# Down projection of a hybrid decoder block: when the weights of its second block of features are loaded and split

## The chip, the cores and the metric

The kernel runs on one core of one Trainium2 chip. The metric is the device time of one execution in microseconds; lower is better. TensorE (PE in the profile) multiplies matrices, VectorE (DVE) and ScalarE (ACT) work on the tiles, GpSimd (POOL) does a few small operations, and SyncE (SP) issues nearly all the transfers. SP is one queue: a transfer whose wait is not yet met holds back every transfer behind it.

## The reference

One decoder block on `x` of 1024 tokens by 1024 features in float32: an attention mixer and a retention mixer read the same normalised input, are gated, merged and projected, and then a squared-ReLU MLP follows. The change lies in the last product of the MLP:

```python
xn2 = rmsnorm(x, norm2_g[l])
x = x + jnp.square(jax.nn.relu(xn2 @ w_up[l])) @ w_down[l]
```

`w_up` is 1024 x 4096 and `w_down` 4096 x 1024.

## The kernel before

**Numbers as pairs.** Each float32 operand is split into a high part (`ACT ACTIVATE`, a copy to fp32r, line 354) and a low part (`DVE TENSOR_TENSOR`, source minus high part, line 357). A product is then three matmuls: high with high, high with low, low with high (line 257).

**The down projection.** The 4096 features are cut into 8 blocks of 512 (`c`, the code's "chunk"), the tokens into 4 pairs of tiles (`t`). A unit `u` is one `(c, t)`, so there are 32 units, four to a block. Each unit is one step of Strassen's scheme: seven products N1 to N7, each of two matmul triples, so 42 matmuls of 128x512. The order in a unit (line 1326) is N6, N5, then N1 of the *next* unit, N7, N2 of the next unit, N3, N4. N1 and N2 of the very first unit stand inside the up projection's last unit (lines 1306 to 1310). In the profile a matmul of the down projection has `xh` or `xl` as its second operand. N1 of blocks 0, 2, 4 and 6 reads the buffer shown as `wh`/`wl`, N1 of blocks 1, 3, 5 and 7 the buffer `y1ah`/`y1al`.

**Rows.** The left operands of a unit, called rows here, were written to DRAM by the up projection (`h_d<-hs`, line 1243) and come back as two transfers of 896 KB, `xh<-h_d` and `xl<-h_d` (`load_rows`, lines 1252 to 1260). Three places rotate, so the rows of unit u+3 are loaded into the place of unit u when unit u has been multiplied. They are first needed at N1 of unit u+3, which stands third in unit u+2.

**Weights.** A block's weights are four quarters of 512 KB (`raw<-in_w_down`, line 210), in four places of their own. From them come the seven operands: three are a quarter itself, four are a sum or a difference of two quarters, made in place (line 186, shown as `raw<-raw,raw`). Each operand is then split into its own buffer. `add_chunks` writes this down as seven steps, in the order N1, N2, N3, N5, N7, N6, N4. The buffers of the even and of the odd blocks are two disjoint sets (lines 400 to 402). Three buffers of the odd set lie in a pool `y1`, opened after the up projection (line 1312), three in a pool `w1` (line 1321).

**Who decides when.** `Weights.pump` writes a step into the program as soon as the buffer that it fills is marked free and its quarters are loaded; `load` writes the load of a quarter as soon as the step that last used the place has been written. `free` marks buffers and calls `pump`. This gives only the order in which the program is *written*. PE keeps that order (line 306). On the other engines, SP's queue included, a planner at compile time orders the instructions: at each point of its own model of time it takes, among those whose inputs and buffers are ready, the one written first. `keep_in_program_order` adds an edge that puts an instruction behind the one written just before it on its engine. After planning, each engine's order is fixed.

**Around the change.** When the last unit of the up projection is done, the loads of block 1's quarters have been written, and opening `y1` and `w1` (lines 1317 and 1324) lets all seven steps of block 1 be written at once, ahead of the loop over the units; the loads of block 2's quarters follow in the same call.

Of the kernel before, what the change touches and what calls it, by code (L numbers as in the profile page):

```python
# [37 lines left out]
class Weights:  # L38
# [9 lines left out]
    RAW = 3  # L48
    A, B, C, D = (0, 1), (2, 3), 5, 4

    def __init__(self, nc, rawp, wp, split):
        self.nc, self.rawp, self.wp, self.split = nc, rawp, wp, split
        self.raw, self.used, self.next = [], set(), 0
        self.src, self.steps = [], []
        self.place, self.more, self.most = [], None, None
        self.last = {}
        self.units, self.done = {}, set()
        self.plain = self.taken = 0
        self.cycle, self.turn = tuple(range(self.WB)), 0

        self.places = {}

    def claim(self, buf, key):

# [105 lines left out]
    def add_chunks(self, tag, srcs, buffers):  # L170


        for c, quarters in enumerate(srcs):
            base = len(self.src)
            self.place += [(base + i) % (self.RAW + 1) for i in range(4)]
            self.src += quarters
            x00, x10, x11, x01 = range(base, base + 4)
            for name, r, other, op, ends in (
                    ("N1", x00, None, None, ()), ("N2", x10, None, None, ()), ("N3", x11, None, None, ()),
                    ("N5", x00, x01, OP.subtract, ()), ("N7", x01, x11, OP.subtract, (x01,)),  # L180
                    ("N6", x11, x00, OP.add, (x00,)), ("N4", x10, x11, OP.subtract, (x10, x11))):
                buf, key = buffers[c % 2][name], (tag, c, name)

                def step(r=r, other=other, op=op, ends=ends, buf=buf, key=key):
                    if other is not None:
                        self.nc.vector.tensor_tensor(self.raw[r], self.raw[r], self.raw[other], op=op)
                    h, l = self.buffer(buf)
                    self.split(h, l, self.raw[r])
                    self.units[key] = h, l
                    self.used.update(ends)  # L190

                self.steps.append((self.claim(buf, key), x01, step))
# [5 lines left out]

    def load(self):
        n = len(self.raw)  # L200
        if n >= len(self.src):
            return False
        b = self.place[n]
        if any(self.place[m] == b and m not in self.used for m in range(max(0, n - 16), n)):
            return False
        from_ = self.rawp if b < self.RAW else self.more if b == self.RAW else self.most
        if from_ is None:
            return False
        raw = from_.tile([P, UW], F, name=f"raw{b}", bufs=1)
        self.nc.sync.dma_start(raw[:, :self.src[n].shape[1]], self.src[n])  # L210
        self.raw.append(raw)
        return True
# [22 lines left out]

    def free(self, *ids):
        self.done.update(ids)
        self.pump()


class Pipe:
# [24 lines left out]
    def step(self, ps, terms, ends=None, first=True):  # L266
        fns = self.due.pop(self.slot, [])
        n, m = len(terms), len(fns)
        place = {}
        for j, fn in enumerate(fns):  # L270
            place.setdefault(min(n - 1, (j + 1) * n // (m + 1)), []).append(fn)

        def after(i):
            for fn in place.get(i, []):
                fn()
            if ends and i in ends:
                ends[i]()

        self.group(ps, terms, after, first)
        self.slot += 1  # L280
# [9 lines left out]
def strassen_order(units):  # L290


    order = [(0, "N1"), (1, "N1"), (0, "N2"), (1, "N2")]
    for j in range(units):
        late = j + 3 >= units
        order += [(j, "N6"), (j, "N5")] + ([] if late else [(j + 2, "N1")]) + [(j, "N7")]
        order += [(j, "N3")]
        order += [(j + 2, "N2")] if not late else [(units - 1, ("N1", "N2")[j + 3 - units])] if j + 1 < units else []
        order += [(j, "N4")]
    return order  # L300
# [3 lines left out]
def hybrid_block(ctx: ExitStack, tc: tile.TileContext, a: dict, out: bass.AP):  # L304
    nc = tc.nc
# [6 lines left out]
    rawp = pool(ctx, "rawp", 1)  # L312
    wp = pool(ctx, "wp", 1)
# [60 lines left out]
        return (slice(0, 512), slice(512, 1024))  # L374


    W = Weights(nc, rawp, wp, split)
    heads = [(slot, g) for slot in range(SLOTS) for g in (1, 2, 0)]
    for u in range(4):
        W.add(a["w_av"][u])  # L380
# [136 lines left out]
    with ExitStack() as ph:  # L517
# [96 lines left out]
        for n, t in enumerate(TILES):  # L614
# [9 lines left out]
            ends = {2 * i + 1: (lambda i=i: W.free(us[i])) for i in range(4)} if n == NT - 1 else None  # L624
            pipe.step(pm, terms, ends)
            c = px.tile([P, 512], F, name="c", bufs=1)
# [59 lines left out]
    for u in range(len(TOKEN)):  # L686
        n1, part = {}, {}
        for name in ("N1", "N2", "N6", "N5", "N3", "N7", "N4"):
            for t in range(4):
# [13 lines left out]
                elif name == "N2":  # L703
                    c = cp.tile([P, 512], F, name="c")
# [409 lines left out]
    with ExitStack() as ph:  # L1114
# [41 lines left out]
        def load_rows(n):  # L1156

            nb, t = order[n]
            ts = slice(t * P, (t + 1) * P)
            xt = pn.tile([P, 512], F, name="xr")  # L1160
            nc.sync.dma_start(xt, a["x"][ts, halves()[nb]])
            y0 = None
            if nb == 1:
                y0 = pn.tile([P, 512], F, name="y0")
                nc.sync.dma_start(y0, out[ts, :512])
            ahead.append((xt, y0))
# [34 lines left out]
    with ExitStack() as ph:  # L1201
# [60 lines left out]
        def down(u, name):  # L1262
# [28 lines left out]
            if t == 3:  # L1291
                W.free(("dn", c, name))

        for j, name in strassen_order(NU):
            product("up", j, name, unit, OP7, temps, result)
            if j == NU - 1:
                if name == "N1":
                    load_rows(0)
                if name == "N2":
                    parts = [x.rearrange("p a b -> p (a b)") for x in OP7[name]]  # L1300
                    for i, part in enumerate("ab"):
                        W.places["n2" + part] = [x[:, 1024 * i:1024 * i + 1024] for x in parts]
                    W.free(("place", "n2"))
                if name == "N5":
                    load_rows(1)
                if name == "N7":
                    down(0, "N1")
                if name == "N3":
                    load_rows(2)
                    down(0, "N2")  # L1310
# [3 lines left out]
        Y.update({r: y1.tile([P, D], F, name=f"Y{r}") for t in (1, 3, 2) for r in (t, t + 4)})  # L1314
        for x in "abc":
            W.places["y1" + x] = [y1.tile([P, UW], R, name=f"y1{x}{i}") for i in "hl"]
        W.free(("place", "y1"))


    with ExitStack() as ph:  # L1320
        w1 = pool(ph, "w1", 1)
        for x in "abc":
            W.places["w1" + x] = [w1.tile([P, UW], R, name=f"w1{x}{i}") for i in "hl"]
        W.free(("place", "w1"))
        for u in range(len(units)):
            for name, later in (("N6", False), ("N5", False), ("N1", True), ("N7", False), ("N2", True),
                                ("N3", False), ("N4", False)):
                if u + later < len(units):
                    down(u + later, name)
            load_rows(u + 3)  # L1330
    sumst.close()


# [106 lines left out]
```

## Time and profile before

| | us |
|---|---|
| median of 3 runs | 2235.59 |
| lowest and highest run | 2232.65 and 2236.57 |
| the profiled execution | 2232.95 |
| its span, first to last instruction | 2231.2 |

The down projection's first product begins at 1898.69 us of the span and the span ends at 2231.2 us. In the views, a row of the timeline is: start in us, duration in us, engine, line, operation, result and operands, count, and in brackets the idle time of the engine before it and what ended that idle time. `SPq` is SyncE issuing a transfer: its duration is the issue, not the transfer. `x` or `w` with an `h` or `l` at the end are the high and low parts.

### The profile page before, as it was taken

The numbers are of one execution on the slowest core, as the hardware profiler recorded it, in microseconds if no ns is written. First come the engines' busy times: TensorE is split into PE (matmuls) and PEld (weight loads), VectorE is DVE, ScalarE is ACT, GpSimd is POOL, SyncE is SP. The second block draws the span as 40 slices with busy tenths as digits, with TensorE's granted clock in tenths as the row PEclk, the third lists the DMA queues.
The fourth block names the chain that finished last, engine by engine and source line by source line (L and its number), as shares of the span: only waits on it lengthen the run. The fifth ranks groups of instructions, "written<-read, shape, count | busy, mean of one in ns | idle before, by whom it ended". The sixth has DMA issues, their size and how long they took to land.

```text
span 2231.2 us, 28546 instructions
## 1 busy us (share of the span) xinstructions
PE 2182.3 (98%) x10064; PEld 1792.3 (80%) x10064; DVE 1435.4 (64%) x2543; ACT 1110.6 (50%) x1936; POOL 196.6 (9%) x184
## 2 busy tenths in 40 slices
PE   8999999999999999999999999999899999899998
PEld 6788788888788887888888788888788888688887
DVE  7766675455555556657767752453877778776863
ACT  6433444477844467745545532122577777522210
POOL 3314453000000000010000000000000000000002
PEclk9999999999999999999999999999999999999999
DMA  7344433544545555364333484554378889966658
GB/s 228 99 132 114 132 114 114 158 145 146 171 149 170 160 155 161 127 207 139 117 102 111 151 283 151 174 180 146 99 223 248 248 248 282 328 248 238 248 223 174
DMA packets 345664, 392.78 MB, mean 176 GB/s; under 512 B 34737, under 2 KB 270897, under 8 KB 345266
## 3 DMA queue, kind: packets, MB, share of 16 engines
q1 hardware_dynamic: 343026, 386.25, 55.0%
q0 software_dynamic: 2496, 4.72, 1.4%
q8 instruction: 79, 1.29, 0.2%
q14 instruction: 63, 0.52, 0.1%
HBM read 252.39 MB, written 138.51 MB: 175 GB/s over the span
## 4 chain that ended last, share of the span: by engine, by line
PE 81%; DVE 6%; ACT 4%; DMA 3%; issue 3%; POOL 2%; SPq 0%; POOLq 0%; ACTq 0%; DVEq 0%
PE mm L257 46%; PE ms L257 29%; DVE wl L357 1%; PE tr L792 1%; PE tr L811 1%; DMA xl<-h_d 1%; DMA raw<-in_w_att_q 1%; ACT wh L354 1%; PE tr L650 1%; DVE xl L357 1%; POOL x L555 1%; PE tr L804 1%; PE ms L934 1%; PE tr L990 1%; ACT xh L354 1%
## 5 line engine op out<-in xcount | busy, mean ns | idle before, releaser
L357 DVE TENSOR_TENSOR wl<-raw,wh 128x1024 fp32r<-128x1024 f32 (+1 forms) x292 | 332.3, 1143 | 175.2 <-ACT wh L354 173.4
L354 ACT ACTIVATE wh<-raw 128x1024 fp32r<-128x1024 f32 (+1 forms) x292 | 287.4, 988 | 253.1 <-PE ms L257 122.1
L257 PE MATMUL mm<-xh,wh 128*128 128x512 f32 x896 | 346.8, 410 | 1.9 <-ACT wh L354 1.2
L257 PE MATMUL mm<-xl,wh 128*128 128x512 f32 x896 | 329.5, 391 | 1.7 <-DVE xl L357 1.7
L257 PE MATMUL mm<-xh,wl 128*128 128x512 f32 x768 | 301.2, 392 | 0.5 <-DVE wl L357 0.5
L257 PE MATMUL mm<-wh,xh 128*128 128x512 f32 x736 | 296.3, 403 | 0.8 <-ACT ms L1279 0.6
L257 PE MATMUL mm<-wh,xl 128*128 128x512 f32 x736 | 288.6, 392 | 4.5 <-DMA xl<-h_d 4.5
L257 PE MATMUL mm<-wl,xh 128*128 128x512 f32 x736 | 287.6, 391 | 0.0
L257 PE MATMUL ms<-xh,wh 128*128 128x512 f32 x544 | 225.6, 415 | 1.8 <-DVE St L981 1.2
L257 PE MATMUL ms<-xh,wl 128*128 128x512 f32 x544 | 212.9, 391 | 0.0
L257 PE MATMUL ms<-xl,wh 128*128 128x512 f32 x544 | 212.4, 390 | 0.0
L257 PEld LDWEIGHTS mm<-xh,wh 128*128 128x128 f32 x896 | 169.2, 189 | 34.4 <-ACT wh L354 1.6
L257 PEld LDWEIGHTS mm<-xl,wh 128*128 128x128 f32 x896 | 169.3, 189 | 31.8 <-DVE xl L357 2.1
L257 PEld LDWEIGHTS mm<-xh,wl 128*128 128x128 f32 x768 | 144.6, 188 | 32.4 <-DVE wl L357 1.0
L257 PEld LDWEIGHTS mm<-wh,xl 128*128 128x128 f32 x736 | 138.4, 188 | 35.1 <-DMA xl<-h_d 5.4
L257 PEld LDWEIGHTS mm<-wh,xh 128*128 128x128 f32 x736 | 138.7, 188 | 27.2 <-ACT ms L1279 1.0
L257 PEld LDWEIGHTS mm<-wl,xh 128*128 128x128 f32 x736 | 138.8, 189 | 25.8
L257 PE MATMUL ms<-wh,xh 128*128 128x512 f32 x336 | 137.0, 408 | 6.0 <-DVE c L705 3.4
L257 PE MATMUL ms<-wh,xl 128*128 128x512 f32 x336 | 133.3, 397 | 2.5 <-DVE xl L357 2.5
L257 PE MATMUL ms<-wl,xh 128*128 128x512 f32 x336 | 132.5, 394 | 0.8 <-DVE wl L357 0.8
L257 PEld LDWEIGHTS ms<-xh,wh 128*128 128x128 f32 x544 | 102.5, 188 | 21.9 <-DVE St L981 1.6
L257 PEld LDWEIGHTS ms<-xh,wl 128*128 128x128 f32 x544 | 102.1, 188 | 22.0
(284 smaller groups left out, 3816.4 us busy)
## 6 DMA issues: line engine op xcount, KB each, us to landing
h_d<-hs SPq DMA_DIRECT2D x112, 512.0 KB, 4.2
xh<-h_d SPq DMA_DIRECT2D x32, 896.0 KB, 6.1
xl<-h_d SPq DMA_DIRECT2D x32, 896.0 KB, 7.3
raw<-in_w_att_q SPq DMA_DIRECT2D x48, 512.0 KB, 4.2
raw<-in_w_up SPq DMA_DIRECT2D x32, 512.0 KB, 3.7
raw<-in_w_down SPq DMA_DIRECT2D x32, 512.0 KB, 5.2
qk_d<-T SPq DMA_DIRECT2D x48, 256.0 KB, 3.5
raw<-in_w_gate_q SPq DMA_DIRECT2D x16, 512.0 KB, 4.4
```

The source lines that it names most:

```text
L257: self.nc.tensor.matmul(ps, x, y, start=start, stop=stop, skip_group_check=not first)
L354: hi = nc.scalar.activation(dst_h, src, AF.Copy)
L357: nc.vector.tensor_tensor(dst_l, src, dst_h.bitcast(F), op=OP.subtract)
L555: nc.gpsimd.tensor_tensor(x[v], x[v], x[u], op=op)
L650: nc.tensor.transpose(pt[:, i, :], c[:, i * P:(i + 1) * P], ident)
L792: nc.tensor.matmul(sp[:, :w], q[:, e * P:(e + 1) * P], k[:, k0 * P:k0 * P + w], start=True, stop=True)
L804: nc.tensor.transpose(tb[:, j * P:(j + 1) * P], st["p"][:, j * P:(j + 1) * P], ident)
L811: nc.tensor.matmul(po[:, :DH], st["t"][:, j * P:(j + 1) * P], v[:, k0 + j, :], start=(j == 0), stop=(j == nk - 1))
L934: nc.tensor.matmul(sp[:, :P], kT[:, f], qT[:, f], start=(f == 0), stop=(f == 1))
L990: nc.tensor.transpose(pt[:, f, :], it["o"][:, f * P:(f + 1) * P], ident)
```

## The change

Four things are changed.

1. While the up projection writes its program, quarters of block 1 and later are not loaded: `limit` is the first quarter of block 1.
2. Opening `y1` and `w1`, and freeing a buffer, no longer writes steps: `eager` is off.
3. In units 1, 2 and 3, after each product, `ease` raises the limit by one quarter (up to the end of block 1) and lets at most one step be written. So the four loads are written after the first four products of unit 1, the steps N1, N2, N3 and N5 after its products 4 to 7, and N7, N6 and N4 after the first three products of unit 2.
4. In the steps of block 1 alone the high part's activation and the sum or difference are kept in program order. The loads and the low part are not.

After unit 3, and behind the loading of the rows of unit 6, limit and `eager` are reset and `pump` runs: block 2's four loads and seven steps are written there at once. From then on everything is as before.

```diff
+        self.limit, self.eager = None, True
+        self.bases = {}
...
         for c, quarters in enumerate(srcs):
-            base = len(self.src)
+            base = self.bases[tag, c] = len(self.src)
...
-                def step(r=r, other=other, op=op, ends=ends, buf=buf, key=key):
+                def step(r=r, other=other, op=op, ends=ends, buf=buf, key=key, pinned=c == 1):
                     if other is not None:
-                        self.nc.vector.tensor_tensor(self.raw[r], self.raw[r], self.raw[other], op=op)
+                        d = self.nc.vector.tensor_tensor(self.raw[r], self.raw[r], self.raw[other], op=op)
+                        if pinned:
+                            self.tc.keep_in_program_order(d)
                     h, l = self.buffer(buf)
-                    self.split(h, l, self.raw[r])
+                    self.split(h, l, self.raw[r], pinned)
...
     def load(self):
         n = len(self.raw)
-        if n >= len(self.src):
+        if n >= (len(self.src) if self.limit is None else self.limit):
             return False
...
     def free(self, *ids):
         self.done.update(ids)
-        self.pump()
+        if self.eager:
+            self.pump()
+
+    def ease(self, last):
+
+        if self.limit is not None:
+            self.limit = min(self.limit + 1, last)
+        self.pump(1)
...
+        W.limit = W.bases["dn", 1]
         for j, name in strassen_order(NU):
             product("up", j, name, unit, OP7, temps, result)
...
+        W.eager = False
         W.free(("place", "y1"))
...
                 if u + later < len(units):
                     down(u + later, name)
+                if 0 < u < 4:
+                    W.ease(W.bases["dn", 2])
             load_rows(u + 3)
+            if u == 3:
+                W.limit, W.eager = None, True
+                W.pump()
```

More of the change, by code (lines that the diff above doesn't have):

```diff
@@ L49, with __init__ @@
     A, B, C, D = (0, 1), (2, 3), 5, 4
-    def __init__(self, nc, rawp, wp, split):
-        self.nc, self.rawp, self.wp, self.split = nc, rawp, wp, split
+    def __init__(self, tc, rawp, wp, split):
+        self.tc, self.nc, self.rawp, self.wp, self.split = tc, tc.nc, rawp, wp, split
         self.raw, self.used, self.next = [], set(), 0
@@ L374, in halves @@
         return (slice(0, 512), slice(512, 1024))
-    W = Weights(nc, rawp, wp, split)
+    W = Weights(tc, rawp, wp, split)
     heads = [(slot, g) for slot in range(SLOTS) for g in (1, 2, 0)]
```

## The prediction

> **What bounds the kernel now.** The page comes first: it says which engine sets the time and where that engine has holes.
>
> ```profile
> span 2231.2 us, 28546 instructions
> ...
> PE 2182.3 (98%) x10064; PEld 1792.3 (80%) x10064; DVE 1435.4 (64%) x2543; ACT 1110.6 (50%) x1936; POOL 196.6 (9%) x184
> ...
> PE   8999999999999999999999999999899999899998
> ...
> DMA  7344433544545555364333484554378889966658
> ```
>
> PE sets the time: it is busy for 98% of the span. So a change is worth what it takes out of PE's holes, or adds to them. A slice is 2231.2 / 40 = 55.8 us. The "8" in slice 34 (from 1897 us, counting from 0) is the start of the down projection, and the DMA row has its highest digits just there and ahead of it. The waits of PE from 1905 us to the end say for what it waits:
>
> ```profile
> PE mm L257 <- DMA xl<-h_d: 6.9, 3, 3.1
> PE ms L257 <- ACT Y L1286: 1.0, 1, 1.0
> ```
>
> Three waits for rows, not for weights. The timeline of PE places them; with the last line of each wait I show the first matmul of N1 of the units 1 to 6, as marks, and a line of the chain of work for the undisturbed pace.
>
> ```profile
> 1910.46 0.39 PE L257 MATMUL mm<-wh,xh 128*128 128x512 f32 x1
> 1921.27 0.39 PE L257 MATMUL mm<-wh,xh 128*128 128x512 f32 x1
> 1924.99 0.50 PE L257 MATMUL mm<-wh,xl 128*128 128x512 f32 x1 [3.11 <-DMA xl<-h_d]
> 1934.57 0.47 PE L257 MATMUL mm<-wh,xh 128*128 128x512 f32 x1 [0.21 <-DMA xh<-h_d]
> 1936.67 0.50 PE L257 MATMUL mm<-wh,xl 128*128 128x512 f32 x1 [1.40 <-DMA xl<-h_d]
> 1947.49 0.39 PE L257 MATMUL mm<-y1ah,xh 128*128 128x512 f32 x1
> 1950.47 0.50 PE L257 MATMUL mm<-y1ah,xl 128*128 128x512 f32 x1 [2.36 <-DMA xl<-h_d]
> 1961.26 0.39 PE L257 MATMUL mm<-y1ah,xh 128*128 128x512 f32 x1
> 1971.27 0.39 PE L257 MATMUL mm<-y1ah,xh 128*128 128x512 f32 x1
> ...
> 1974.16 2.72 PE mm L257 x12
> ```
>
> Twelve matmuls take 2.72 us, so a product of six takes 1.36 us and a unit of 42 takes 9.52 us. From N1 to N1 the units took 10.81, 13.30, 12.92, 13.77 and 10.01 us. What is above 9.52 is lost: 1.29, **3.78 (stall 1, rows of unit 2), 3.40 (stall 2, rows of unit 3), 4.25 (stall 3, rows of unit 4)** and 0.49; in all 13.21 us. After 1971 us the chain is PE alone until its tail. Why the rows are late stands in SP's timeline:
>
> ```profile
> 1907.96 1.14 SPq L210 DMA_DIRECT2D raw<-in_w_down  x1
> 1909.19 0.53 SPq L1259 DMA_DIRECT2D xh<-h_d  x1
> ...
> 1916.46 1.09 SPq L1259 DMA_DIRECT2D xl<-h_d  x1
> ...
> 1919.81 6.09 SPq L210 DMA_DIRECT2D raw<-in_w_down  x3
> 1926.00 0.38 SPq L1259 DMA_DIRECT2D xh<-h_d  x1
> 1926.47 0.51 SPq L1259 DMA_DIRECT2D xl<-h_d  x1
> 1931.44 0.32 SPq L1259 DMA_DIRECT2D xh<-h_d  x1
> 1938.39 5.43 SPq L210 DMA_DIRECT2D raw<-in_w_down  x4
> 1943.92 0.38 SPq L1259 DMA_DIRECT2D xl<-h_d  x1
> ...
> SPq L210 <- DVE raw L186: 8.7, 2, 6.6
> ```
>
> The quarters of block 1 are the raw loads at 1907.96 (one) and 1919.81 (three), those of block 2 the four at 1938.39. Stall 2: the rows of unit 3 could be asked for when N4 of unit 0 is done, two products ahead of 1921.27, so near 1918.6, but the three raw loads hold SP until 1925.9. Stall 3: the rows' high part for unit 4 goes at 1931.44; then SP waits 6.6 us (last row, the waits of SP) for DVE to be done with a sum of block 1, issues four raw loads, and only then the low part, 12.5 us after the high one. Stall 1: the low part for unit 2 stands behind stores of the up projection's last results (left out here) which wait for DVE; one raw load went ahead of them.
>
> **The change part by part.**
>
> *Stall 3 goes: 4.25 us.* Block 2's four loads are now written behind the loading of the rows of unit 6, so rows of units 4, 5 and 6 that are ready come first. And their places are freed by block 1's steps N7, N6 and N4, now written in unit 2, whereas the rows of unit 4 are asked for at the end of unit 1. The low part then follows its high part by some 0.4 us, as in the pair at 1926, is issued near 1932 and needed 12.2 us later (nine products of 1.36 us); even the 8.5 us that the low part of 1916.46 took (to 1924.99) would do. I take 4.25; the ends are 0 and 4.25.
>
> *Stall 2 goes: 3.40 us.* Three loads leave the place ahead of the rows of unit 3. If they are issued where they are written, in unit 1, SP is free near 1919.8 and the pair goes some 6 us earlier, against waits of 0.21 + 1.40 us and what they bring behind them. Ends 0 (loads still early, first rival) and 3.40. I take 3.40, because the rows of unit 3 need only be first by 2 us.
>
> *Stall 1: no change.* The low part is held by the stores, which the change doesn't touch. If the load at 1907.96 is gone, 512 KB less lie ahead of it. The windows give the price:
>
> ```profile
> 1908.00:1936.00 28.00, 22.95 (x98) 17.76 (x96) 15.37 (x21) 16.71 (x27) 0.00 (x0) 1.00 1.04 348
> 1936.00:1941.00 5.00, 4.33 (x12) 3.43 (x13) 5.00 (x5) 2.79 (x4) 0.00 (x0) 0.66 0.47 175
> ...
> 1920.20:1923.60 3.40, 1.68 (x8) 1.06 (x6) 0.00 (x0) 1.10 (x2) 0.00 (x0) 1.00 0.99 326
> ...
> 1933.80:1937.20 3.40, 1.78 (x7) 0.91 (x6) 3.12 (x4) 2.49 (x3) 0.00 (x0) 1.00 0.92 371
> 1937.20:1940.60 3.40, 3.40 (x9) 2.63 (x8) 3.40 (x4) 1.54 (x2) 0.00 (x0) 0.51 0.33 120
> ```
>
> Columns are the window, its length, busy time of PE, PEld, DVE, ACT and POOL, then granted clock, DMA share and GB/s. From 1908 to 1936 the transfers are full (share 1.04) at 348 GB/s, so 512 KB are 1.5 us; behind that, SP's waits leave them half idle (0.47), which is where room for the moved loads comes from. Bounds: a gain of 3.78 (stall gone) to a loss of 1.67, explained next. I take 0, nearest to the row of the low part, whose issue does not move.
>
> The loss is the clock. Each of the other two stalls is followed by a stretch of 3.4 us at a granted clock of 0.51 (last two rows): 3.4 x 0.49 = 1.67 us, part of the 3.40 and the 4.25 above. It came after a window with PE busy for 1.78 of 3.40 us; after the window at 1920.20, with 1.68 us, it didn't come. So a stall 1 that stays may cost one more such stretch. [...]
>
> *Loads of block 1 in unit 1: 0.* Four times 512 KB, one per product. They now lie ahead of the rows of unit 4: 2 MB at 348 GB/s are 6.0 us, the rows themselves (1.8 MB) 5.3 us, in all 11.3 of the 12.2 us. Cover is thin; if it is gone, the cost is 1 us or, with the slow stretch, 2.7.
>
> *Steps of block 1 in units 1 and 2, pinned on ACT and DVE: 0.* The same 7 activations, 7 low parts and 4 sums as before, later. Unit prices from a later, undisturbed part:
>
> ```profile
> 1994.33 1.23 DVE L357 TENSOR_TENSOR w1al<-raw,w1ah 128x1024 fp32r<-128x1024 f32 x1 [0.41 <-ACT w1ah L354]
> ...
> 1995.59 0.33 SPq L210 DMA_DIRECT2D raw<-in_w_down  x1
> ...
> 1998.79 1.22 DVE L186 TENSOR_TENSOR raw<-raw,raw 128x1024 f32<-128x1024 f32 x1
> 1999.92 0.68 DVE L1288 TENSOR_TENSOR Y<-Y,ms 128x512 f32<-128x512 f32 x1
> 2000.04 4.93 SPq L210 DMA_DIRECT2D raw<-in_w_down  x3
> 2000.04 1.06 ACT L354 ACTIVATE w1bh<-raw 128x1024 fp32r<-128x1024 f32 x1 [3.02 <-DVE raw L186]
> 2000.52 1.22 DVE L186 TENSOR_TENSOR raw<-raw,raw 128x1024 f32<-128x1024 f32 x1
> ...
> DMA to landing us min/median/max: 3.9/5.0/10.2
> ```
>
> An activation is 1.06 us, a low part 1.23, a sum 1.22 and a result added to Y 0.68. The edge adds a wait on ACT: behind a pinned activation whose quarter has not landed stand the copies of N1's result (line 1279), and N2 waits for those, one product (1.36 us) after N1. The first step is written three products (4.1 us) after its load, which lands in 5.0 us in the middle case and 10.2 at the most (last row, the view of the raw tiles). A wait of 0.9 us is hidden by that product, one of 6.1 would cost 6.1 - 1.4 = 4.7. I take 0, by the middle case. The first use of the block is N1 of unit 4, third in unit 3, over a unit after the last step: nothing waits there.
>
> *Block 2 all at once after unit 3: 0.* Seven steps are 7 x 1.23 + 4 x 1.22 = 13.5 us of DVE; a unit's six results are 4.1 of its 9.52 us. Block 2 is first needed at N1 of unit 8, 3.3 units or 31 us later, where DVE has 31 - 13 = 18 us free. The rows above show a like burst with results of Y between the steps and PE undisturbed. The bad end is the rival below.
>
> **Sum.** -3.40 - 4.25 = -7.65 us. On the profiled execution that is 2232.95 - 7.65 = 2225.3 (its span 2231.2 and 1.75 around it). That execution lies 2.64 us below the median of the runs, 2235.59; from the median the forecast is 2227.94, so **2228**.
>
> **Rivals.**
>
> *The loads don't move.* Loads are not pinned, and SP's order is not the written one. In the rows above, the load at 1995.59 leaves just after the low part of N7 (to 1995.56) frees its place, 4.5 us ahead of three loads of which at least one, that into the place freed by N6's sum at 1999.92, was written before it. Block 1's places are free before unit 1, so its loads can still go ahead of the rows of unit 3. Against it: they now are written behind those rows, and the stores left out between SP's rows were written ahead of them too. Then stall 2 stays and 4.25 us are gained: 2231.3, or up to 1.2 us less since block 1's first low part (1.23 us) no longer stands ahead of the last stores: 2231.
>
> *The next rows are late instead.* Block 1's 2 MB meet the rows of unit 4 and stall 3 comes back whole, for the thin cover named above; only 3.40 are gained: 2232.2. For it speaks the full DMA share until 1936, against it the half idle time behind.
>
> *Slower: DVE's queue is filled with block 2 at the end of unit 3.* If the planner, trusting early landings, puts the eleven operations of block 2 ahead of unit 4's results, N7 waits for N6's result, with only two products (2.7 us) between: 13.5 - 2.7 = 10.8 us, and up to 10.2 more for the last quarter's landing, on which N5's difference waits; I take half of that, 5. Net +15.9 - 7.65: 2243.8. It is slower by 0.2% from 12.1 us on (7.65 + 4.5). Against it stands the mixing in the rows above; but there the quarters had landed long before.
>
> **How the numbers follow.** Forecast 0.50, loads that don't move 0.25, next rows late 0.13, slower 0.12. The range: 2224 is the forecast with stall 1 gone too (2227.9 - 3.8); upward it takes in the first two rivals and stops short of the slower one, which is left out: 2234. A measurement of this kernel can tell about 0.2%, 4.5 us, from no change. Faster by that: the forecast, less 0.03, and a little over half of the first rival, 0.61. Within: the rest of these two and the second rival, 0.27. Slower: 0.12.
>
> **What would show it.** Right: SP's timeline has the two parts of the rows of units 3 and 4 back to back, raw loads behind them; the waits of PE on `xl<-h_d` shrink from 6.9 us to stall 1's 3.1; granted clock 1.00 from 1930 on; N1 to N1 is 9.5 us from unit 3 on. Wrong: three or four raw loads in one piece ahead of the rows of unit 3 (first rival), a wait for `xl` at N1 of unit 4 (second), or waits of PE on `DVE Y` or `ACT ms` in units 2 to 5 (pins, or block 2's burst).

## The result, and the profile after

| | before | after |
|---|---|---|
| median | 2234.64 us (20 runs, 2230.43 to 2239.49) | 2230.41 us (20 runs, 2225.44 to 2236.36) |
| ratio | | 0.9981, 95% interval 0.9974 to 0.9987 |
| profiled execution | 2232.95 us | 2233.11 us |
| its span | 2231.2 us | 2231.0 us |

The change gains 4.2 us of the 7.65 that were forecast, 0.19%. The interval is clear of 1, but the gain is just under the 4.5 us (0.2%) that the prediction took as the least that can be told from no change. The two profiled executions are equally long all the same, so the page alone shows nothing. The page of the kernel after:

```profile
span 2231.0 us, 28539 instructions
...
PE   8899999999999999999999999999999999999998
```

The slice that held an "8" at the start of the down projection (34, counting from 0) now has a "9". To see more, the down projection is measured by itself, from the start of its first matmul to the start of its last. The timeline of PE, kernel before, its last matmul:

```profile
2223.49 0.39 PE L257 MATMUL ms<-w1ch,xl 128*128 128x512 f32 x1
```

From 1898.69 that is 324.80 us. The timeline of PE of the kernel after has the first matmul, the first one of N1 of units 1 to 7, every first matmul after a long wait from unit 1 on, and the last matmul. All line numbers of the kernel after stand 11 higher there: L268 is the matmul, L1290 the copy of N1's result, L1299 a result added to Y.

```profile
1902.18 0.39 PE L268 MATMUL mm<-wh,xh 128*128 128x512 f32 x1
...
1913.34 0.39 PE L268 MATMUL mm<-wh,xh 128*128 128x512 f32 x1
...
1924.14 0.39 PE L268 MATMUL mm<-wh,xh 128*128 128x512 f32 x1
...
1926.14 0.50 PE L268 MATMUL mm<-wh,xl 128*128 128x512 f32 x1 [1.38 <-DMA xl<-h_d]
...
1935.39 0.39 PE L268 MATMUL mm<-wh,xh 128*128 128x512 f32 x1
...
1944.92 0.39 PE L268 MATMUL mm<-y1ah,xh 128*128 128x512 f32 x1
...
1949.33 0.50 PE L268 MATMUL mm<-y1bh,xh 128*128 128x512 f32 x1 [1.53 <-ACT ms L1290]
...
1956.27 0.39 PE L268 MATMUL mm<-y1ah,xh 128*128 128x512 f32 x1
...
1965.79 0.39 PE L268 MATMUL mm<-y1ah,xh 128*128 128x512 f32 x1
...
1970.40 0.50 PE L268 MATMUL ms<-w1ah,xh 128*128 128x512 f32 x1 [3.10 <-DVE Y L1299]
...
1976.14 0.50 PE L268 MATMUL ms<-w1ch,xh 128*128 128x512 f32 x1 [1.22 <-DVE Y L1299]
...
1980.35 0.39 PE L268 MATMUL mm<-y1ah,xh 128*128 128x512 f32 x1
...
2223.09 0.39 PE L268 MATMUL ms<-w1ch,xl 128*128 128x512 f32 x1
```

The down projection takes 2223.09 - 1902.18 = 320.9 us, 3.9 less than before. It starts 3.5 us later in this execution, which is why the spans agree. This sets one execution against one: the kernel before was profiled once, and a second profile of the change, below, gives 321.8.

As in the prediction, what is above 9.52 us from N1 of one unit to N1 of the next is lost. The columns are the unit from whose N1 the time runs (2, 3 and 4 hold the prediction's stalls 1, 2 and 3):

| lost, us | 0 | 1 | 2 | 3 | 4 | 5 | 6 |
|---|---|---|---|---|---|---|---|
| before | 2.25 | 1.29 | 3.78 | 3.41 | 4.25 | 0.49 | 0 |
| after | 1.63 | 1.29 | 1.72 | 0.02 | 1.82 | 0 | 5.05 |

Both waits for rows at units 3 and 4 are gone and the one at unit 2 is smaller. Two new waits have come, one at unit 4 for ACT and one for DVE in column 6; that one is at N7 and N4 of unit 5, which stand behind N1 of unit 6. The view of the waits of PE has the same four (the wait for `Y` of ACT is in unit 0 and was there before):

```profile
PE ms L268 <- DVE Y L1299: 4.3, 2, 3.1
PE mm L268 <- ACT ms L1290: 1.5, 1, 1.5
PE mm L268 <- DMA xl<-h_d: 1.4, 1, 1.4
PE ms L268 <- ACT Y L1297: 1.0, 1, 1.0
```

SP's timeline, kernel after, shows why the rows now come in time, and when block 2's quarters leave:

```profile
1918.54 1.33 SPq L1270 DMA_DIRECT2D xl<-h_d  x1
...
1922.24 4.09 SPq L1270 DMA_DIRECT2D xh<-h_d  x1
1926.42 0.45 SPq L1270 DMA_DIRECT2D xl<-h_d  x1
1926.92 1.86 SPq L214 DMA_DIRECT2D raw<-in_w_down  x4
1932.63 0.33 SPq L1270 DMA_DIRECT2D xh<-h_d  x1
1933.06 0.62 SPq L1270 DMA_DIRECT2D xl<-h_d  x1
...
1950.08 1.47 SPq L214 DMA_DIRECT2D raw<-in_w_down  x2
...
1957.06 0.87 SPq L214 DMA_DIRECT2D raw<-in_w_down  x2
```

The rows of unit 3 go at 1922.24 and 1926.42, then block 1's four quarters in one piece, then both parts of the rows of unit 4 back to back. No raw load holds up rows that are ready. Block 2's quarters leave two at a time, when block 1's low parts (`w1al` to 1950.05, `w1cl` to 1957.03) free their places; the first two leave ahead of the rows of unit 6 (issued at 1953.51), behind which they are written. As in the kernel before, a load is not held where it is written.

The new waits stand in the timelines of ACT and DVE of the kernel after. ACT first:

```profile
1947.74 1.06 ACT L365 ACTIVATE w1ah<-raw 128x1024 fp32r<-128x1024 f32 x1 [1.94 <-DVE raw L188]
1948.70 0.58 ACT L1290 ACTIVATE ms<-mm 128x512 f32<-128x512 f32 x1
...
1965.16 1.06 ACT L365 ACTIVATE wh<-raw 128x1024 fp32r<-128x1024 f32 x1 [4.17 <-DMA raw<-in_w_down]
```

```profile
1966.26 1.22 DVE L368 TENSOR_TENSOR wl<-raw,wh 128x1024 fp32r<-128x1024 f32 x1 [2.30 <-ACT wh L365]
1967.40 1.22 DVE L188 TENSOR_TENSOR raw<-raw,raw 128x1024 f32<-128x1024 f32 x1
1968.53 1.22 DVE L368 TENSOR_TENSOR wl<-raw,wh 128x1024 fp32r<-128x1024 f32 x1
1969.67 0.68 DVE L1299 TENSOR_TENSOR Y<-Y,ms 128x512 f32<-128x512 f32 x1
```

At unit 4 a step of block 1 (`w1ah`) waits 1.94 us for its sum, and the copy of N1's result, for which PE waits at 1949.33, stands behind it. At 1965.16 the third quarter of block 2 has landed, 8.1 us after its issue began (the fourth follows 1.3 us later); DVE has waited 2.30 us for its high part, and three operations of block 2 stand ahead of the result at 1969.67 that PE waits for until 1970.40.

### The profile page after: what moved, and what is told of

The parts are those of the page before. It is cut to its first block, busy times and chain, and to the rows that moved or that the text cites. A ratio compares the mean times of both kernels' runs of the same rounds, so it can differ in the third digit from the quotient of the medians.

```text
span 2231.0 us, 28539 instructions
## 1 busy us (share of the span) xinstructions
PE 2181.1 (98%) x10064; PEld 1791.4 (80%) x10064; DVE 1433.8 (64%) x2543; ACT 1109.0 (50%) x1936; POOL 201.2 (9%) x184
## 3 DMA queue, kind: packets, MB, share of 16 engines
q8 instruction: 79, 1.29, 0.2%
## 4 chain that ended last, share of the span: by engine, by line
PE 78%; DVE 7%; DMA 5%; ACT 5%; issue 3%; POOL 2%; SPq 0%; POOLq 0%; ACTq 0%; DVEq 0%
PE mm L268 45%; PE ms L268 28%; DVE wl L368 2%; DMA raw<-in_w_att_q 1%; PE tr L803 1%; PE tr L822 1%; ACT wh L365 1%; PE tr L661 1%; DVE xl L368 1%; POOL x L566 1%; DMA xl<-h_d 1%; PE tr L815 1%; PE ms L945 1%; PE tr L1001 1%; ACT xh L365 1%
## 5 line engine op out<-in xcount | busy, mean ns | idle before, releaser
L268 PE MATMUL mm<-xh,wh 128*128 128x512 f32 x896 | 346.3, 410 | 1.5 <-ACT wh L365 1.5
L268 PE MATMUL mm<-xl,wh 128*128 128x512 f32 x896 | 329.2, 391 | 1.7 <-DVE xl L368 1.7
L268 PE MATMUL mm<-xh,wl 128*128 128x512 f32 x768 | 301.0, 392 | 0.5 <-DVE wl L368 0.5
L268 PE MATMUL mm<-wh,xh 128*128 128x512 f32 x736 | 296.6, 403 | 0.0
L268 PE MATMUL mm<-wh,xl 128*128 128x512 f32 x736 | 288.3, 392 | 1.4 <-DMA xl<-h_d 1.4
L268 PE MATMUL mm<-wl,xh 128*128 128x512 f32 x736 | 287.4, 391 | 0.0
L268 PE MATMUL ms<-xh,wh 128*128 128x512 f32 x544 | 226.2, 416 | 2.0 <-DVE St L992 1.2
L268 PE MATMUL ms<-xl,wh 128*128 128x512 f32 x544 | 212.8, 391 | 0.7 <-DVE xl L368 0.7
L268 PE MATMUL ms<-xh,wl 128*128 128x512 f32 x544 | 213.2, 392 | 0.0
L268 PEld LDWEIGHTS mm<-xh,wh 128*128 128x128 f32 x896 | 169.1, 189 | 33.7 <-ACT wh L365 1.9
L268 PEld LDWEIGHTS mm<-xl,wh 128*128 128x128 f32 x896 | 169.0, 189 | 31.7 <-DVE xl L368 2.1
L268 PEld LDWEIGHTS mm<-xh,wl 128*128 128x128 f32 x768 | 144.2, 188 | 31.9 <-DVE wl L368 1.0
L268 PEld LDWEIGHTS mm<-wh,xl 128*128 128x128 f32 x736 | 138.3, 188 | 31.7 <-DMA xl<-h_d 1.8
L268 PEld LDWEIGHTS mm<-wl,xh 128*128 128x128 f32 x736 | 138.9, 189 | 25.8
L268 PEld LDWEIGHTS mm<-wh,xh 128*128 128x128 f32 x736 | 138.6, 188 | 26.2 <-ACT ms L1290 0.4
L268 PE MATMUL ms<-wh,xh 128*128 128x512 f32 x336 | 137.9, 410 | 7.6 <-DVE c L716 4.9
L268 PE MATMUL ms<-wh,xl 128*128 128x512 f32 x336 | 134.7, 401 | 2.4 <-DVE xl L368 2.4
L268 PE MATMUL ms<-wl,xh 128*128 128x512 f32 x336 | 134.0, 399 | 1.2 <-DVE ss L381 0.8
L268 PEld LDWEIGHTS ms<-xh,wh 128*128 128x128 f32 x544 | 102.6, 189 | 23.3 <-DVE St L992 1.6
L268 PEld LDWEIGHTS ms<-xh,wl 128*128 128x128 f32 x544 | 102.2, 188 | 21.8
```

The costliest lines, as they stand in the source:

```text
L268: self.nc.tensor.matmul(ps, x, y, start=start, stop=stop, skip_group_check=not first)
```

## The experiments

The theory after the result: what was gained are the rows, and what was given back are two places where a block's splitting stands ahead of work that PE needs. The rivals: the pins do it; or late quarters cost the same wherever they are split. All measured values first, by kernel. "Length" is that of the down projection in the one execution profiled, the numbered columns are lost us as above, blank is under 0.25. The ratio is worked out from all runs and is not the quotient of the two medians. Left out are columns 0 and 1, which hold 1.36 to 2.21 and 1.02 to 1.35 in every kernel, and columns 5, 8 and 12, in which "limit only" lost 0.49 (5), "block 2 apart" 0.65 (8) and "three apart again" 0.31 (12).

| kernel | median (before) | ratio, interval | length | 2 | 3 | 4 | 6 | 7 | 9 |
|---|---|---|---|---|---|---|---|---|---|
| no pins | 2232.65 (2234.92) | 0.9996 [0.9987, 1.0005] | 322.9 | 1.71 | | 1.82 | 6.86 | | |
| block 2 spread | 2231.02 (2234.92) | 0.9992 [0.9982, 1.0002] | 319.5 | 2.88 | | 1.85 | 3.07 | | |
| limit only | 2233.61 (2234.92) | 0.9998 [0.9987, 1.0009] | 323.4 | 4.47 | 4.52 | 2.20 | | | |
| spread, pinned | 2228.74 (2234.92) | 0.9980 [0.9972, 0.9989] | 320.1 | 1.90 | | 1.82 | 3.71 | | |
| block 2 apart | 2235.45 (2233.56) | 1.0013 [1.0004, 1.0022] | 325.0 | 1.57 | | 1.87 | | | 8.53 |
| both apart | 2228.86 (2233.56) | 0.9979 [0.9970, 0.9988] | 319.7 | 1.65 | | | 0.31 | 4.76 | |
| block 2 later | 2229.72 (2233.56) | 0.9984 [0.9974, 0.9994] | 321.1 | 1.61 | | | | | 6.77 |
| three apart | 2223.52 (2233.44) | 0.9958 [0.9943, 0.9974] | 314.6 | 1.71 | 0.25 | | | | |
| three apart, no pins | 2226.22 (2233.44) | 0.9967 [0.9954, 0.9980] | 316.0 | 1.65 | | 1.83 | | | |
| the change again | 2229.33 (2232.83) | 0.9983 [0.9970, 0.9995] | 321.8 | 1.81 | | 1.88 | 5.39 | | |
| three apart again | 2225.14 (2232.83) | 0.9960 [0.9943, 0.9976] | 314.1 | 1.58 | | | | | |

A column holds a wait and what a slower clock lost beside it, and the second part differs from run to run. For the columns of the two blocks the parts are these; the waits are PE's for results that DVE adds to `Y`, and 0.50 is the granted clock:

| kernel | column | lost, us | waits, us | clock during and behind the wait |
|---|---|---|---|---|
| the change | 6 | 5.05 | 3.10 and 1.22 | 1.00 |
| no pins | 6 | 6.86 | 4.26 | 0.50 for 6.8 us |
| block 2 spread | 6 | 3.07 | 2.74 | 1.00 |
| spread, pinned | 6 | 3.71 | 1.84 | 0.50 for 3.4 us |
| the change again | 6 | 5.39 | 3.42 | 0.50 for 3.4 us |
| both apart | 7 | 4.76 | 2.86 | 0.50 for 3.4 us |
| block 2 apart | 9 | 8.53 | 6.86 | 0.50 for 6.8 us |
| block 2 later | 9 | 6.77 | 4.10 | 0.50 for 6.8 us |

**No pins.** The change without its fourth part:

```diff
-                def step(r=r, other=other, op=op, ends=ends, buf=buf, key=key, pinned=c == 1):
+                def step(r=r, other=other, op=op, ends=ends, buf=buf, key=key, pinned=False):
```

> The change without its pins: block 1's loads and steps are written where the change writes them, but neither the activations nor the sums are kept in program order. Theory (pins): with the pins each sum stands behind the low part of the step before, which makes a chain of 3.5 us per step, and ACT waits at its head for that chain with N1's copy of unit 4 behind it; without pins the 1.82 us lost between N1 of unit 4 and N1 of unit 5 go, and block 1 is done earlier. Rival (landing): block 1's quarters land near 1936 us, later than the planner thought, and its work piles up ahead of the results with or without pins; then between 1 and 3 us are still lost there. Both: stalls 2 and 3 stay away (under 0.5 us lost between N1 of unit 3 and N1 of unit 4); first to last matmul of the down projection 319 us (theory) or 321 us (rival), against 320.9 with the change and 324.8 before.

The wait at unit 4 is the same 1.5 us. ACT's timeline of this kernel:

```profile
1949.10 1.06 ACT L365 ACTIVATE w1bh<-raw 128x1024 fp32r<-128x1024 f32 x1 [1.00 <-DVE raw L188]
1950.06 0.58 ACT L1290 ACTIVATE ms<-mm 128x512 f32<-128x512 f32 x1
```

Now two activations of block 1 stand ahead of the copy instead of one. The pins are not the cause of this wait: with or without them the copy stands behind, as the rival had it (its length, 321, was too low). The crowd at block 2 is one wait now:

```profile
PE mm L268 <- DVE Y L1299: 4.3, 1, 4.3
```

That is as much as the change waited there in two pieces. The larger loss (6.86 against 5.05) is the clock, at 0.50 for 6.8 us, of which 4.9 us lie behind the wait. In the medians no gain is left that is clear of noise.

**Block 2 spread.** Block 2's loads and steps are let go one per product in units 4 and 5 instead of all at once:

```diff
-                if 0 < u < 4:
-                    W.ease(W.bases["dn", 2])
+                if 0 < u < 6:
+                    W.ease(W.bases["dn", 2 if u < 4 else 3])
...
-            if u == 3:
+            if u == 5:
                 W.limit, W.eager = None, True
                 W.pump()
```

> The change, and block 2 written one piece per product too, in units 4 and 5, not pinned; the limit falls at the end of unit 5. Theory: where a load or a step is written doesn't place it; as soon as its place or its quarter is free it goes, so block 2's work still stands on DVE ahead of unit 5's results and 3 to 5 us are lost between N1 of unit 6 and N1 of unit 7 (5.05 with the change); first to last matmul 320 to 321 us. Rival: writing all of block 2 at once makes the crowd; written one by one, under 1 us is lost there and first to last matmul takes 316.5 us.

The loss in column 6 goes from 5.05 to 3.07, not to nothing, as the theory had it; the clock stays at 1.00 in both, and the wait alone goes from 4.32 to 2.74. So the burst has a part in it, and writing one step per product does not end it.

**Limit only.** The loads of block 1 are held back during the up projection alone; everything else is as before the change:

```diff
-        W.eager = False
+        W.limit = None
         W.free(("place", "y1"))
...
-                if 0 < u < 4:
-                    W.ease(W.bases["dn", 2])
             load_rows(u + 3)
-            if u == 3:
-                W.limit, W.eager = None, True
-                W.pump()
```

> Of the change only the limit during the up projection: block 1's quarters are not loaded before the up projection is written to its end; then everything is let go at once, as before the change, without pins. Theory: the one early load of block 1 (at 1907.96 us before) and block 1's first split were what the change took from stall 1, which goes from 3.78 to about 1.7 us; four raw loads now stand ahead of the rows of unit 3 and four ahead of the second part of unit 4's rows, so stalls 2 and 3 stay, together 7 to 9.5 us. First to last matmul 323 to 325 us. Rival: stall 1 shrank for another reason (another landing order in that one execution) and stays at 3.5 us or more; 325 to 327 us.

SP's timeline of this kernel, and PE's at N1 of unit 3:

```profile
1922.29 5.62 SPq L214 DMA_DIRECT2D raw<-in_w_down  x4
1928.01 0.38 SPq L1270 DMA_DIRECT2D xh<-h_d  x1
```

```profile
1938.14 0.47 PE L268 MATMUL mm<-wh,xh 128*128 128x512 f32 x1 [2.56 <-DMA xh<-h_d]
...
1940.25 0.80 PE L268 MATMUL mm<-wh,xl 128*128 128x512 f32 x1 [1.41 <-DMA xl<-h_d]
```

With the four loads written ahead of the loop they leave ahead of the rows of unit 3, and that wait is back, larger; behind it the clock was at 0.50 for 6.8 us, which is a part of the 4.52. The wait at N1 of unit 2 itself was 1.44 us, as in the change: for the smaller stall 1 it is enough that no load leaves during the up projection. Stalls 2 and 3 need the rest: that loads and steps are written inside the units. The pins have no part in it, since without them both stalls stayed away.

**Spread, pinned.** Block 2 spread as above, and its activations and sums kept in program order too (`pinned=c in (1, 2)`).

> As the run with block 2 written one piece per product in units 4 and 5, but with block 2's activations and sums kept in program order as block 1's are. Theory: what crowds DVE is work put ahead of results because the planner takes quarters as landed; pinned behind the results of units 4 and 5 it can't stand ahead of them, and the 5.05 us between N1 of unit 6 and N1 of unit 7 go to under 1 us; the 1.82 us of block 1's pins stay; first to last matmul 316 to 317 us, 2226 us in all. Rival: DVE has simply too much to do there (it is busy for over 95% from 1966 to 1978 us with the change); then 3 us or more are lost, there or one to three units later.

3.71 us stay, not the less than 1 us of the theory: a wait of 1.84 us, and most of the rest is the clock behind it. The quarters of block 2 leave SP at 1950.49 and 1957.47, and the last ones land from 1963.1 on; behind that DVE does a sum and three low parts (1964.28 to 1968.83) ahead of the result for which N7 of unit 5 waits. A pin orders the steps; it does nothing for steps written ahead of the landing.

**Block 2 apart; both apart; block 2 later.** So the steps were written at set products, later than the landing. A flag was added to `ease`, and a list of (unit, product) at which one step may be written; the loads are let go at every product:

```diff
-                def step(r=r, other=other, op=op, ends=ends, buf=buf, key=key, pinned=c == 1):
+                def step(r=r, other=other, op=op, ends=ends, buf=buf, key=key, pinned=c in (1, 2), held=c in (1, 2)):
...
-                        if pinned:
+                        if held:
                             self.tc.keep_in_program_order(d)
...
-    def ease(self, last):
+    def ease(self, last, step=True):
...
-        self.pump(1)
+        while self.load():
+            pass
+        if step:
+            self.pump(1)
...
+        STEPS = ((1, 4), (1, 5), (1, 6), (1, 7), (2, 1), (2, 2), (2, 3),
+                 (4, 7), (5, 3), (5, 5), (5, 7), (6, 3), (6, 5), (6, 7))
...
-                if 0 < u < 4:
-                    W.ease(W.bases["dn", 2])
+                if 0 < u <= 6:
+                    W.ease(W.bases["dn", 2 if u < 4 else 3], (u, p) in STEPS)
...
-            if u == 3:
+            if u == 6:
                 W.limit, W.eager = None, True
                 W.pump()
```

This is "block 2 apart", with block 1 where the change has it, and with the activations (`pinned`) and the sums (`held`) of both blocks kept in program order. The other two keep only the activations of both blocks (`held=c in ()`). "Block 2 later" has block 1 at `(2, 1), (2, 3), (2, 5), (2, 7), (3, 3), (3, 4), (3, 6)` and block 2 as here; "both apart" has that block 1, block 2 at `(4, 5), (4, 7), (5, 1), (5, 3), (5, 5), (5, 6), (5, 7)`, and lets go after unit 5.

> Block 1 exactly as in the change. Block 2's loads are released one per product from unit 4 on, and its seven steps are written one by one at set products from the end of unit 4 to the end of unit 6, with the activation and the sum kept in program order. Theory (crowding: the 5.05 us lost around unit 5 in the change come from the eleven DVE operations of block 2 standing in one piece ahead of results): the waits of PE on Y in units 5 and 6 sink under 1 us in all; the 1.5 us wait at N2 of unit 4 for N1's copy stays, since block 1 is untouched; the down projection takes some 317 us (320.9 in the change) and the whole about 2226.5. Rival (block 2's late landing or DVE's capacity sets it): 3 us or more are lost in units 5 to 8 wherever the steps stand, 2229 or more; the loss may then stand where block 3 follows, in units 7 and 8.

> Both blocks re-spaced: block 1's steps after products 1, 3, 5 and 7 of unit 2 and 3, 4 and 6 of unit 3 (loads as in the change), block 2's after products 5 and 7 of unit 4 and 1, 3, 5, 6 and 7 of unit 5; only the activations of both blocks are kept in program order, the sums are not. Theory (the 1.8 us at unit 4 are lost because an activation of block 1 that waits for its sum stands ahead of the copy of N1's result on ACT, and the 5.05 us at unit 5 because results stand behind block 2's work on DVE): both go to under 0.7 us; what stays is stall 1 (1.3 to 1.9 us) and the starts; the down projection takes 314.5 to 316.5 us and the whole is 2223 to 2226. Rival (late landings set it, not the order): N6 or N7 of unit 4 waits for block 1's last operands, or units 5 to 8 lose 3 us as before: 2228 or more.

> Block 1 as in the kernel with both blocks re-spaced, block 2 later: after product 7 of unit 4 and then every other product to the end of unit 6; activations kept in program order. Theory (order): as there, both waits under 0.7 us, the down projection 314.5 to 317 us, but block 3 now follows closer and may cost up to 1.5 us around units 7 and 8; 2223 to 2227. Rival (landing): no wait on Y in unit 5, since block 2 has landed by then, but 3 us or more in units 7 and 8.

All three lengths are above the theories' (325.0 against 317, 319.7 against 316.5 at most, 321.1 against 317 at most), and in each the 3 us or more of the rival are lost, though not always in its units. Three things came out. First, with block 1's steps moved the loss in column 4 goes from 1.87 (block 2 apart) to 0.07 (both others). Its quarters land no earlier there: block 1's first activation starts 22.7 us behind N1 of unit 1 in "both apart" and 23.0 in the change. But the sums of block 1 are no longer pinned either, and no run moves the steps and leaves the sums pinned, or the other way round; the share of each is open. Second, with block 2 spread from the end of unit 4 to the end of unit 6 nothing is lost in columns 6 and 7; written closer, seven steps over ten products instead of fifteen ("both apart"), it loses 4.76: the last quarters landed from 1962.4 on, and from 1963.5 to 1979.7 DVE worked without a pause, with sums and low parts in pairs ahead of results. Third, the loss did not go, it moved: to column 9, where block 3 is split, which is now the first block let go whole with its quarters landing late. DVE's timeline of "block 2 apart" there:

```profile
1991.88 0.68 DVE L1302 TENSOR_TENSOR Y<-Y,ms 128x512 f32<-128x512 f32 x1
1992.80 1.23 DVE L371 TENSOR_TENSOR y1bl<-raw,y1bh 128x1024 fp32r<-128x1024 f32 x1 [0.24 <-ACT y1bh L368]
...
2001.88 1.23 DVE L371 TENSOR_TENSOR w1bl<-raw,w1bh 128x1024 fp32r<-128x1024 f32 x1
2003.02 0.69 DVE L1302 TENSOR_TENSOR Y<-Y,mm 128x512 f32<-128x512 f32 x1
```

Between the two results, 11 us apart, DVE does nine operations of block 3 (low parts, L371 in this kernel, and sums, L188) and no result; PE waits 6.86 us of them. "Block 2 apart" is 0.13% slower than before, and the loss stands where block 3 follows, which its rival had named as possible; the theory had named the cause of column 6 and missed that block 3 inherits it.

**Three apart.** To "block 2 later" block 3 is added, at `(8, 1), (8, 3), (8, 5), (8, 7), (9, 3), (9, 5), (9, 7)`, and the activations of blocks 1 to 3, not their sums, are kept in program order; from block 4 on all is as before. "Three apart, no pins" is the same with nothing kept in program order.

```diff
-                if 0 < u <= 6:
-                    W.ease(W.bases["dn", 2 if u < 4 else 3], (u, p) in STEPS)
+                if 0 < u <= 9:
+                    W.ease(W.bases["dn", 2 if u < 4 else 3 if u < 7 else 4], (u, p) in STEPS)
...
-            if u == 6:
+            if u == 9:
```

> The kernel with block 2 later, and block 3 treated likewise: its seven steps after products 1, 3, 5 and 7 of unit 8 and 3, 5 and 7 of unit 9, activations of blocks 1 to 3 kept in program order; from block 4 on as before. Theory (the loss is the burst of the first block whose steps are all free to run when its quarters land; each block that is spread passes it to the next): the 6.8 us at block 3 go, block 4's buffers come free one per product as in the kernel before, so nothing is lost after it; only stall 1 (1.3 to 1.9 us) and the starts stay; the down projection takes 314 to 315.5 us, the whole 2221 to 2225. Rival (late quarters cost the same wherever they are split): 3 us or more are lost again at block 3 or 4, in units 8 to 12, 318 us or more.

> The same places in the program for the steps of blocks 1, 2 and 3, with nothing kept in program order. Theory (the place of a step in the program alone does not hold it, since the planner takes what is ready first in its own time; with the activations held the low parts follow them): without pins the low parts and sums come closer together and 2 us or more are lost at block 2 or 3; the down projection takes 317 us or more. Rival (place alone is enough, the pins do nothing): within 0.7 us of the same kernel with pins, 314 to 316 us.

The waits of PE from 1895 us on, "three apart" (the wait for `u` is the up projection's):

```profile
PE mm L271 <- DMA xl<-h_d: 1.4, 1, 1.4
PE ms L271 <- ACT u L443: 1.4, 1, 1.4
PE ms L271 <- ACT Y L1300: 1.0, 1, 1.0
PE mm L271 <- ACT ms L1293: 0.3, 1, 0.3
```

No wait for a result that DVE adds to `Y` is left, and nothing over 0.2 us is lost in columns 4 to 13. The theory held, with 0.9958 of before. The same work of blocks 2 and 3, spread out, costs nothing here, so neither DVE's load as a whole nor the late landing alone makes the loss. Without pins the rival was nearly right: place alone ends the crowds on DVE, but 1.83 us are lost at unit 4 again. The medians of the two, from five runs each, do not part them (their intervals overlap); the column does. ACT's timelines, with pins and then without:

```profile
1949.69 0.58 ACT L1293 ACTIVATE ms<-mm 128x512 f32<-128x512 f32 x1 [0.75 <-PE mm L271]
1950.18 1.05 ACT L368 ACTIVATE w1ah<-raw 128x1024 fp32r<-128x1024 f32 x1
```

```profile
1943.36 1.06 ACT L368 ACTIVATE w1bh<-raw 128x1024 fp32r<-128x1024 f32 x1 [1.00 <-DVE raw L188]
1944.32 0.58 ACT L1293 ACTIVATE ms<-mm 128x512 f32<-128x512 f32 x1
```

Written behind the copy and pinned there, the activations of block 1 leave N1's result alone; written there and not pinned, they get ahead of it. It takes both, the place and the pins on the activations.

**Both once more, on one chip.**

> The change itself once more, on the chip on which the kernel with three blocks apart runs next, for a direct comparison and for a second look at its waits. All theories: the lost times fall at the same places as in its first profile, since the order on each engine is fixed: about 1.8 us at unit 4 and 5 us at unit 5, the down projection near 320.9 us, the ratio to before within 0.9974 to 0.9987.

> The kernel with blocks 1 to 3 apart once more, beside the change. Theory: the down projection again takes some 314.6 us, 6 us less than the change, and the medians differ by 5 to 7 us. Rival (the part ahead of the down projection varies by as much from run to run and hides it): under 3 us between the medians.

The change lost at the same places (1.88 and 5.39). The down projection of "three apart" is 7.7 us shorter than the change's here, the medians are 4.2 apart: less than expected, more than the rival allowed. In the profiled executions a part of the gain is taken back ahead of the stage: the down projection of "three apart" began at 1904.7 and 1903.9 us, against 1902.2 and 1900.7 in the change. Whether that holds for the other runs, and why, is open.

## Why the prediction was right, and where it was wrong

2230.4 lies in the range, 2.4 us above the forecast, and the two terms that made the sum were right. It was nearer than its steps deserved, and that was luck: two terms put at 0 cost 6.9 us, and another term put at 0, with two columns that the sum left out (0 and 5), gave 3.2 back. The starting point moved too: the forecast counted from 2235.59, the median of three runs, and over 20 runs the kernel before has 2234.64, so of the gain 3.4 us are missing. With 4.2 us the gain falls, by the prediction's own 4.5, in the outcome "within", which had 0.27 against 0.61 for faster. By columns: -7.65 + 1.82 + 5.05 - 2.06 - 0.62 - 0.49 = -3.95, and the down projection became 3.9 us shorter.

- *Stall 3 goes: 4.25.* Right in size and way: the two parts of the rows of unit 4 leave back to back (1932.63, 1933.06), and N1 of unit 4 has no wait for them. The cover was thin: the low part landed 11.5 us after its issue, near 1944.6, and was read at 1945.38, 0.8 us later. What stands in that column now is another wait, below.
- *Stall 2 goes: 3.40.* Right: 3.39, but with less room than the "some 6 us" of the prediction. Counted from N1 of unit 1, the low part of unit 3's rows was issued at 13.1 us (1926.42 - 1913.34) instead of 16.0 (1926.47 - 1910.46), 2.9 earlier; it landed 8.7 us later, near 1935.1, and was read at 1935.84. The rival "loads don't move" fell, though its premise held: block 1's loads went in one piece and not where each was written, but behind the rows of unit 3, which were ready. Limit only is that rival's picture and has its stall.
- *Stall 1: no change.* Mis-sized: 2.06 less. The low part's issue counted from N1 of unit 1 came at 5.20 us (1918.54 - 1913.34) instead of 6.00 (1916.46 - 1910.46), and it landed 7.6 us after that instead of 8.5. The size varies: with "block 2 spread", whose program is written alike up to there, the wait was 2.59 us instead of 1.38. The prediction had the price, 1.5 us for the 512 KB ahead, and left it out since the issue seemed fixed. The slow stretch of the clock behind it, the other end, did not come: the granted clock was 1.00 from 1908 to 1962 us of the kernel after.
- *Loads of block 1 in unit 1: 0.* Right: no rows were late for them, so the second rival fell too, by the 0.8 us above.
- *Steps of block 1, pinned: 0.* Mis-sized: 1.82. The step priced a wait for a landing quarter; ACT's wait for the first one was 0.2 us, although the quarters landed 9.4 to 11.8 us after their issue and not in the middle case's 5.0. What cost was a wait for a sum: a difference, its high part and its low part follow each other across two engines, 3.5 us a step, with the copy of N1's result behind. The pins alone were not the cause (no pins: the same 1.82); the steps ahead of that copy were. Written later, with the activations pinned and the sums free, they cost nothing (three apart), and written later without pins they cost 1.83 again.
- *Block 2 all at once after unit 3: 0.* This is the step that failed: 5.05. It was argued from the rows around 1994, where a like burst ran between results; but there the quarters had landed long before, which the prediction itself held against those rows under its "slower" rival, and took 0 all the same. SP's timeline, kernel before:

```profile
1965.59 1.56 SPq L210 DMA_DIRECT2D raw<-in_w_down  x2
```

These are the last of that block, issued 17 us ahead of its first step (its activation at 1982.85, its low part at 1984.32). In the changed kernel block 2's quarters leave when block 1's low parts free their places, at 1950 and 1957, the last two land from 1965.16 on, and eight of the block's eleven DVE operations follow from 1966.26 on. That is the mechanism of the "slower" rival, DVE's queue filled ahead of results, one unit later than it was placed (at N7 of unit 5, not of unit 4) and at a third of its 15.9 us: not eleven operations stood ahead of one result, but at most three, behind a wait of 2.30 us.

That the crowd comes from the block being let go whole, behind a late landing, is shown by its moving: with block 2 spread behind its landing it appears at block 3, and with block 3 spread too it is gone. Why the planner puts a block's work ahead of results in that case is open.

## What to carry to other kernels

When loads are delayed to let something more urgent pass, the work that hangs on them can turn into a burst (here block 2's, 5.05 us): look for the first block whose data land after its buffers are free, and spread its work over the products behind the real landing, until a block is reached whose buffers come free one by one. With a planner that takes what is ready, a step's place in the program does not hold it (here 1.83 us were lost at unit 4 without the pins), so work ahead of which something urgent must stand has to be written behind it and also kept there. Where the rest of a kernel varies by as much as the change, compare the stage from its first to its last instruction.

## What was not expected of the hardware

The slow clock after a stall. Windows of PE, laid by the stalls (columns as in the prediction): the change, run again, then "both apart", then the change's first profile:

```profile
1966.47:1969.87 3.40, 0.00 (x1) 0.00 (x1) 3.40 (x5) 2.03 (x3) 0.00 (x0) 1.00 0.65 266
1969.87:1973.27 3.40, 3.40 (x9) 2.62 (x10) 3.40 (x4) 1.06 (x1) 0.00 (x0) 0.54 0.38 95
```

```profile
1974.60:1978.00 3.40, 0.56 (x3) 0.13 (x1) 3.40 (x5) 2.53 (x3) 0.00 (x0) 1.00 0.96 392
1978.00:1981.40 3.40, 3.39 (x9) 2.66 (x10) 2.37 (x3) 1.06 (x1) 0.00 (x0) 0.55 0.83 239
```

```profile
1970.40:1973.80 3.40, 3.40 (x14) 2.67 (x15) 3.40 (x4) 1.06 (x1) 0.00 (x0) 1.00 0.38 84
```

Stalls of 3.42 and 2.86 us were followed by 3.4 us at 0.54 and 0.55, nine matmuls instead of fourteen; the stall of 3.10 us before the last row was followed by full clock. In "spread, pinned" a stall of 1.84 us was followed by 3.4 us at 0.50; in "block 2 spread" one of 2.74 us was not. So among these five stalls, of 1.84 to 3.42 us, the length does not decide, and the change had such a stretch behind this stall in its second profile and none there in its first. In the three stalls above 4 us (4.26, 6.86 and 4.10) the clock fell before the stall ended and stayed at 0.50 for 6.8 us: in "block 2 apart", whose stall is the 6.86 us, it was 0.57 from 1999.40 to 2002.80 us with PE busy for 0.00 us, then 0.50 to 2006.20 us and 0.93 in the 3.4 us after that. At 0.54 a stretch of 3.4 us takes 1.6 us (3.4 x 0.46), but not all of that need be lost: in the change again column 6 is only 0.34 us longer than at first, since PE, slower, had the wait of 3.42 us for `Y` alone and not the 1.22 us for the next result.
